# Two-layer hybrid decoder trunk on one core: gate-weight split inside the fixed first stage, a later gate chain, a value sum in SBUF, and convolutions without edge operations

## The chip, the cores and the metric

The kernel runs on one core of a Trainium2 chip. The metric is the device time of one execution in microseconds. Engines are named as in the profile: PE (TensorE matmul), PEld (its weight loads), DVE (VectorE), ACT (ScalarE), POOL (GpSimd), SP (SyncE, which issues most DMAs). L12 is line 12 of the kernel before the change.

## The reference, cut to what matters

Sequence 1024, model width 1024, two layers, all in float32. In each layer:

```python
shift, scale, gate = split(silu(c) @ w_ada + b_ada, 3)
h = rmsnorm(x, norm_g) * (1 + scale) + shift
mq, mk, mv, mo, mz, mi, mf, rq, rk, rv, rz = split_cols(h @ w_in)
qk = silu(causal_dwconv(concat(mq, mk), conv_w, conv_b))      # 4 taps along the sequence
y_m = sigmoid(mo) * layernorm(mlstm(qk, mv, mi + b_i, mf + b_f)) * silu(mz)   # 4 heads of 256
y_r = layernorm(retention(rotary(rq), rotary(rk), rv)) * silu(rz)             # 4 heads of 256
x = x + gate * (concat(y_m, y_r) @ w_out)
```

`mi` and `mf` are the input and forget gates: four columns each, 8 of the 9224 columns of `w_in`. A running maximum over the sequence of their cumulated logarithms scales the mLSTM heads. A final rmsnorm follows.

## The kernel before

**Precision.** Every float32 operand is split into a high part (a cast on ACT, `high` L399 or `split_to` L854) and a low part (a subtraction on POOL or DVE, `low` L404 or L855), and a product is three matmuls (`mm3`, L173 to L175).

**First stage.** The hidden rows `hT` are made tile by tile (8 tiles of 128 model columns, two halves of 512 tokens) and used at once by three blocks of 128 columns (`first`, L1473 to L1477). In layer 0 a script of short steps (L1481 to L1490) fixes the order of all engines: S, Q square sums of x; K scaling; T transposes; A one accumulation of the adaptive weights `w_ada` on DVE (L285, L287; A13 is group 1, row tile 3); P column sums; G gain and shift from them (L268 to L271); H the high part of a hidden tile (L1515, ACT), E its full value (L1521, ACT), U its low part (L1525, DVE); F and f the products with the high and the low part; W, w the split of weights. The loads of x, of the four groups of `w_ada` (L277) and of the three blocks stand on SP's queue in the order of use, and behind the last of them the gate weights (`gate_raw`, L476, tile `wgr`).

**Gates.** Behind the first stage `gate_units` (L480) makes the gate weights into a 36-column block: two zero fills (L485) and two high parts (L854) on ACT, two low parts (L855) on DVE, tiles cH and cL; then 48 matmuls. `gate_chain` (L495) turns the result into decays: some ACT functions, then 30 instructions of 4x512 on DVE (all of them, like the rotary tables', are shown as L140), eight transposes on PE (L554), and small work.

**Second stage, in slots.** The other columns go in pairs of blocks by Strassen's scheme with seven products, a11, S1, S2, a12, S4, S3, a22. `build_forms` (L612) makes the sums of hidden tiles that they need: U1 to U3 in four steps and, five ticks after the last of these, U4 in four more (L618 to L639, splits at L854 and L855). A pair of value heads (job v) has 14 slots, each product in two parts, in the order a12, a11, S2, S1, S3, a22, S4; a pair of z, query or key columns has 7 slots. The order of the jobs is the string `plan`. In a value pair (`vpair_product`, L769) the bank of a12 (pz, two of them) gets a11's product added (L803), and a store (L772) reads it from there: high part on ACT (L774), low part on DVE (L779), DMA. S1 takes the same two banks next. ACT copies of products (L754, L802, L808), sums and stores use twelve tiles named acc. Query and key pairs of the mLSTM heads go through `conv_chain` (L857): a scaled copy on ACT (L861), three multiply-adds on DVE (L867), for the second half of the tokens three more over the first 1 to 3 columns (L869) with the last three columns of the first half (`halo`, L863), then SiLU. Retention pairs are rotated (L940 to L942).

**What sets the order.** PE's order is the program's. On ACT, DVE, POOL and SP a planner lays each engine's order down when the program is built, by modelled times, and may take an instruction ahead of others that were written before it; it may also take one that was written behind the first stage into it. `late` pins an instruction behind what is written before it on its engine. Side work is written as generators that run in ticks, one tick per slot; `launch(gen, d)` starts one d ticks later and `yield n` puts it off by n. `gate_units` takes two ticks, the block behind it four, then slot 0 follows. The gate chain starts in the third tick and waits 7 ticks; its DVE work takes ten ticks, and its transposes come 13 ticks after the first of them. The attention of a head is launched 4 ticks after its keys, is one at a time, and lets the next one begin after 22 ticks (RELEASE, L964).

Of the kernel before, what the change touches and what calls it, by code (L numbers as in the profile page):

```python
# [19 lines left out]
P = 128  # L20
# [67 lines left out]
def tile_hybrid_trunk(ctx, tc, x, xt, c, positions, w_ada, b_ada, norm_g, w_in, w_blk, w_val, conv_w, conv_b,  # L88
# [16 lines left out]
    def nm(s):  # L105
        uid[0] += 1
        return f"{s}_{uid[0]}"
# [4 lines left out]
    def wt(tag, n, bufs, dt=F32):  # L112
        return wrk.tile([P, n], dt, tag=tag, bufs=bufs, name=nm(tag))

# [15 lines left out]
    def f(ap):  # L130
        return ap.bitcast(F32)

    def late(ins):
        tc.keep_in_program_order(ins)
        return ins
# [604 lines left out]

    def pair_product(F, done, loose=False):
        bank, keep = {}, {}

        def product(n, part, w):
            b, form = PRODUCT[n]
            new = b not in bank
            if new:
                bank[b] = ps_x() if b == "X" else ps_z()
            for k in range(4):
                mm3(bank[b], w[k], F[form][k], new and k == 0, k == 3, b != "Y")  # L750
            with tc.high_priority():
                if n in ("a11", "S1", "S2"):
                    keep[n] = wt("acc", 512, NACC)
                    A.copy(keep[n], bank[b])  # L754
                elif n == "a12":
                    c = keep["a11"] if loose else bank["Y"]
                    V.tensor_tensor(c, bank["Y"], keep["a11"], ALU.add)
                    done(0, 0, c)
                elif n == "S3":
                    V.tensor_tensor(keep["S1"], bank["X"], keep["S1"], ALU.add)  # L760
                    done(1, 1, keep["S1"])
                elif n == "S4":
                    V.tensor_tensor(keep["S2"], bank["Z"], keep["S2"], ALU.add)  # L763
                    done(0, 1, keep["S2"])
                else:
                    done(1, 0, bank["X"])
        return product

    def vpair_product(l, F, heads):  # L769
# [15 lines left out]
        def product(n, part, w):  # L785
# [13 lines left out]
            with tc.high_priority():  # L799
                if n == "a11":  # L800
                    c = wt("acc", 512, NACC)
                    A.copy(c, bank["X"])  # L802
                    V.tensor_tensor(bank["Y"], bank["Y"], c, ALU.add)  # L803
# [52 lines left out]

    def conv_chain(l, hg, which, m, half, pt, halo):  # L857
        cl = cols[l][0]
        ct = which * 8 + hg * 2 + m
        acc = wt("acc", 512, NACC)  # L860
        A.activation(acc, pt, AF.Identity, bias=cl[:, 8 + ct:9 + ct], scale=cl[:, 72 + ct:73 + ct])  # L861
        if half == 0:
            V.tensor_copy(halo, pt[:, HALF - 3:HALF])  # L863
        yield 1
        for d in range(1, 4):
            wcol = cl[:, 24 + 16 * (3 - d) + ct:25 + 16 * (3 - d) + ct]
            V.scalar_tensor_tensor(acc[:, d:], pt[:, 0:HALF - d], wcol, acc[:, d:], ALU.mult, ALU.add)  # L867
            if half:
                V.scalar_tensor_tensor(acc[:, 0:d], halo[:, 3 - d:3], wcol, acc[:, 0:d], ALU.mult, ALU.add)  # L869
        yield 1  # L870
# [46 lines left out]
    def conv_done(l, hg, which):  # L917
        halos = [wt("halo", 3, 4) for _ in range(2)]
        late = []

        def one(m, half, src, delay=0):
            launch(conv_chain(l, hg, which, m, half, src, halos[m]), delay)

        def done(m, half, src):
            if m and half:
                late.append(src)
                return
            one(m, half, src)
            if m:
                one(1, 1, late[0], 1)  # L930
        return done
# [425 lines left out]
    def norm_later(l, xn, sq, hT, half, keep, gaps):  # L1357
# [97 lines left out]
    for l in range(DEPTH):  # L1455
# [23 lines left out]
        if l == 0:  # L1479
# [10 lines left out]
            for step in script.split():  # L1490
# [59 lines left out]
            head_cols(0, hrows)  # L1550
            startup.__exit__(None, None, None)
        else:
            for half in range(2):
                for k in range(KT):
                    first(half, k)
                    tick()
                if half == 0:
                    drain()
        for half in range(2):
            z_evac(gp, 0)(half, pf[0][half])  # L1560
            o_evac(gp, 0, gdr[l][0])(half, pf[1][half])
            z_evac(gp, 1)(half, pf[2][half])
        if l == 0:
            for r in ring3:
                A.activation(r[:, :, HD:HD + 2], ident[:, 0:8].rearrange("p (a c) -> p a c", a=4), AF.Copy, scale=0.0)
                A.copy(r[:, 0:2, HD:HD + 1], rmask[:, 254:256].unsqueeze(2))
# [12 lines left out]
        plan = ("v45 v67 z4 q4 k4 z5 q5 k5 v01 q6 k6 q7 z6 k7 q0 a10 k0 v23 q1 k1 a11 q2 k2 q3 a20 k3 z7 a21 a30 a31",  # L1579
                "v45 q4 k4 z4 q5 k5 v67 q6 k6 z5 q7 k7 v01 q0 k0 z6 a10 q1 k1 v23 q2 k2 a11 q3 k3 a20 z7 a21 a30 a31")[l]  # L1580
        jobs = [(w[0], [int(d) for d in w[1:]]) for w in plan.split()]
# [17 lines left out]
        def job_product(what, arg):  # L1599
# [10 lines left out]
            if h > 3:  # L1610
                return pair_product(F, rot_done(l, h, which, *rot), True)
            return pair_product(F, conv_done(l, h, which))

# [86 lines left out]
```

## Time and profile before

| | |
|---|---|
| median of 3 runs | 2282.63 us (2281.71 to 2287.09) |
| the profiled execution | 2286.23 us |
| its span, first to last instruction | 2284.5 us |
| its granted PE clock, mean | 0.972 |
| busy: PE, DVE, ACT, POOL | 93%, 80%, 50%, 42% |
| DMA, mean | 196 GB/s |

The profile is one execution. Its waits name who ended an engine's idle time; a wait for several things is put down to the last. Rows of the timeline read: start and length in microseconds from the span's start, engine, line, operation, output<-inputs, shapes, count, and in brackets the idle time before it with who ended it. Rows by groups read: busy microseconds, mean nanoseconds of one, idle time before them.

### The profile page before, as it was taken

The page shows a single profiled execution, that of the slowest core. Times are in us where ns is not written, and L with a number is a line of the kernel's source. Part 1 is how long each engine was busy: PE and PEld are TensorE (multiplying, and loading weights), DVE is VectorE, ACT ScalarE, POOL GpSimd, SP SyncE. Part 2 cuts the span into 40 slices and gives each one's busy share as a digit, 9 for nine tenths or more (in the row PEclk, how much of TensorE's full clock was granted, in tenths as well). Part 3 has the DMA queues.
Part 4 walks back from the last instruction along what each step waited for, and adds up shares of the span by engine and source line. Part 5 has one row for each costly group of instructions (what it writes and reads, how often), then busy time and mean ns, then how long its engine had stood idle before and what let it go on. Part 6 is the DMA issues. An engine that isn't in the chain of part 4 may idle for free. (4 is left out here: it accounts for less than half of the span.)

```text
span 2284.5 us, 35248 instructions
## 1 busy us (share of the span) xinstructions
PE 2134.0 (93%) x11483; PEld 1840.7 (81%) x11483; DVE 1827.6 (80%) x3301; ACT 1150.6 (50%) x2157; POOL 957.2 (42%) x842
## 2 busy tenths in 40 slices
PE   5979899999999998999999799999999899899998
PEld 3778789878897877888787788988988888688887
DVE  5898888888979999893627989698697789977653
ACT  5634344444555656653456333544555555565442
POOL 0343244444354544514266434544635353442323
PEclk8999999999999999999999899999999999999999
DMA  8247678887686767686633676877867677576974
GB/s 261 66 116 217 192 233 228 237 240 190 180 244 166 191 183 188 194 268 212 215 126 79 201 197 194 245 193 204 245 159 207 183 205 196 155 205 198 261 256 118
DMA packets 452549, 448.32 MB, mean 196 GB/s; under 512 B 191218, under 2 KB 309754, under 8 KB 452364
## 3 DMA queue, kind: packets, MB, share of 16 engines
q1 hardware_dynamic: 432636, 410.14, 58.0%
q0 software_dynamic: 19584, 35.66, 10.4%
q8 instruction: 90, 1.47, 0.3%
q14 instruction: 95, 0.78, 0.1%
q10 hardware_dynamic: 144, 0.26, 0.0%
HBM read 322.69 MB, written 123.24 MB: 195 GB/s over the span
## 5 line engine op out<-in xcount | busy, mean ns | idle before, releaser
L399 ACT CAST wH<-R 128x512 fp32r<-128x512 f32 x616 | 378.2, 618 | 463.7 <-PE px L174 122.1
L404 POOL TENSOR_TENSOR R<-R,wH 128x512 fp32r<-128x512 f32 x276 | 395.9, 1441 | 508.1 <-ACT wH L399 344.2
L173 PE MATMUL px<-b,wH 128*128 128x512 f32 x912 | 365.1, 400 | 11.1 <-ACT acc L754 8.2
L174 PE MATMUL px<-b,wH 128*128 128x512 f32 x912 | 362.7, 398 | 0.0
L175 PE MATMUL px<-b,R 128*128 128x512 f32 x912 | 361.7, 397 | 0.0
L404 DVE TENSOR_TENSOR R<-R,wH 128x512 fp32r<-128x512 f32 x340 | 258.4, 764 | 112.3 <-ACT wH L399 107.5
L174 PE MATMUL pz<-b,wH 128*128 128x512 f32 x704 | 276.2, 392 | 5.1 <-DVE b L1251 5.1
L173 PE MATMUL pz<-b,wH 128*128 128x512 f32 x704 | 276.6, 393 | 1.9 <-DVE acc L763 1.8
L175 PE MATMUL pz<-b,R 128*128 128x512 f32 x704 | 275.3, 391 | 0.0
L173 PEld LDWEIGHTS px<-b,wH 128*128 128x128 f32 x912 | 176.0, 193 | 49.3 <-ACT acc L754 10.2
L175 PEld LDWEIGHTS px<-b,R 128*128 128x128 f32 x912 | 175.6, 193 | 38.4
L174 PEld LDWEIGHTS px<-b,wH 128*128 128x128 f32 x912 | 175.9, 193 | 34.1
L173 PE MATMUL px<-wH,b 128*128 128x256 f32 (+1 forms) x576 | 176.3, 306 | 18.3 <-DVE acc L867 6.3
L693 POOL DMA_DIRECT2D R<-in_w_blk_dram x104 | 92.4, 889 | 207.7 <-DMA R<-in_w_blk_dram 90.6
L174 PE MATMUL px<-R,b 128*128 128x256 f32 (+1 forms) x576 | 174.6, 303 | 4.2 <-DVE R L404 4.2
L175 PE MATMUL px<-wH,b 128*128 128x256 f32 (+1 forms) x576 | 174.2, 302 | 0.0
L174 PEld LDWEIGHTS pz<-b,wH 128*128 128x128 f32 x704 | 132.9, 189 | 31.4 <-DVE b L1251 6.4
L175 PEld LDWEIGHTS pz<-b,R 128*128 128x128 f32 x704 | 132.9, 189 | 28.4
L173 PEld LDWEIGHTS pz<-b,wH 128*128 128x128 f32 x704 | 132.9, 189 | 28.3 <-DVE acc L763 2.2
L173 PE MATMUL pz<-wH,b 128*128 128x256 f32 (+1 forms) x448 | 135.8, 303 | 17.3 <-DVE acc L779 16.0
L175 PE MATMUL pz<-wH,b 128*128 128x256 f32 (+1 forms) x448 | 135.2, 302 | 0.7 <-DVE b L1251 0.7
L174 PE MATMUL pz<-R,b 128*128 128x256 f32 (+1 forms) x448 | 135.1, 302 | 0.0
(359 smaller groups left out, 5346.7 us busy)
## 6 DMA issues: line engine op xcount, KB each, us to landing
R<-in_w_blk_dram SPq DMA_DIRECT2D x276, 256.0 KB
vdr<-acc SPq DMA_DIRECT2D x128, 256.0 KB
ring<-vdr SPq DMA_DIRECT2D x64, 512.0 KB
R<-in_w_out_dram SPq DMA_DIRECT2D x128, 256.0 KB
R<-in_w_blk_dram POOLq DMA_DIRECT2D x104, 256.0 KB, 4.5
R<-in_w_val_dram SPq DMA_DIRECT2D x80, 256.0 KB
gdr<-acc SPq DMA_DIRECT2D x64, 256.0 KB
acc<-in_w_ada_dram SPq DMA_DIRECT2D x64, 256.0 KB
```

The lines of the kernel that those rows point to most:

```text
L173: PE.matmul(o, lt[0], rt[0], start=start, stop=False, skip_group_check=more)
L174: PE.matmul(o, lt[0], rt[1], start=False, stop=False, skip_group_check=more)
L175: PE.matmul(o, lt[1], rt[0], start=False, stop=stop, skip_group_check=more)
L399: A.copy(h, r)
L404: eng.tensor_tensor(lo, r, f(h), ALU.subtract)
L693: G.dma_start(raw[n], src, accum_op=ALU.add)
```

## The change

1. The split of the gate weights becomes a function of its own, `gate_weights`. In layer 0 it is step X of the fixed first stage, between f04 and U05; in layer 1 it stands behind the first half's products, pinned, and its load ahead of them.
2. `gate_chain` waits 12 ticks instead of 7, and layer 1's plan has z4 ahead of q4 and k4.
3. In a value pair the sum of a12 and a11 is written to the acc tile of a11's copy instead of the bank, and the store reads it there.
4. The kept tiles of a pair have three more columns in front; the halo is copied there, so that the convolution's three multiply-adds run over the second half in one piece and L869 goes. All acc tiles are 516 columns instead of 512.
5. Small: the fills of the value ring's last columns are pinned behind the first stage, the products of `norm_later` are pinned in the first half, and `late` does nothing inside the fixed first stage.

```diff
     def wt(tag, n, bufs, dt=F32):
-        return wrk.tile([P, n], dt, tag=tag, bufs=bufs, name=nm(tag))
+        t = wrk.tile([P, 516 if tag == "acc" else n], dt, tag=tag, bufs=bufs, name=nm(tag))
+        return t[:, 0:n] if tag == "acc" else t
...
-    def gate_units(gr, hT, pgs):
+    def gate_weights(gr):
         wg = (wt("cH", 516, 1, F32R)[:, 0:KT * 36], wt("cL", 516, 1, F32R)[:, 0:KT * 36])
...
         for w in w3:
-            A.activation(w[:, :, 4:32], ones.unsqueeze(1).to_broadcast([P, KT, 28]), AF.Copy, scale=0.0)
+            late(A.activation(w[:, :, 4:32], ones.unsqueeze(1).to_broadcast([P, KT, 28]), AF.Copy, scale=0.0))
         for a, b in ((0, 4), (32, 0)):
-            split_to((w3[0][:, :, a:a + 4], w3[1][:, :, a:a + 4]), gr3[:, :, b:b + 4], V)
+            late(A.copy(w3[0][:, :, a:a + 4], gr3[:, :, b:b + 4]))
+            late(V.tensor_tensor(w3[1][:, :, a:a + 4], gr3[:, :, b:b + 4], f(w3[0][:, :, a:a + 4]), ALU.subtract))
+        return wg
+
+    def gate_units(wg, hT, pgs):
...
-        yield 7
+        yield 12
...
+        def halo(n, pt):
+            if conv:
+                V.tensor_copy(full[n][:, 0:3], pt[:, HALF - 3:HALF])
...
                 if n in ("a11", "S1", "S2"):
-                    keep[n] = wt("acc", 512, NACC)
+                    full[n] = wt("acc", 515, NACC)
+                    keep[n] = full[n][:, 3:515]
...
-                    V.tensor_tensor(bank["Y"], bank["Y"], c, ALU.add)
-                    launch(store(part, 0, 0, bank["Y"]))
-                    del bank["Y"]
+                    V.tensor_tensor(c, bank["Y"], c, ALU.add)
+                    launch(store(part, 0, 0, c))
...
-    def conv_chain(l, hg, which, m, half, pt, halo):
+    def conv_chain(l, hg, which, m, half, pt):
...
-        if half == 0:
-            V.tensor_copy(halo, pt[:, HALF - 3:HALF])
...
-            V.scalar_tensor_tensor(acc[:, d:], pt[:, 0:HALF - d], wcol, acc[:, d:], ALU.mult, ALU.add)
-            if half:
-                V.scalar_tensor_tensor(acc[:, 0:d], halo[:, 3 - d:3], wcol, acc[:, 0:d], ALU.mult, ALU.add)
+            e = 0 if half else d
+            V.scalar_tensor_tensor(acc[:, e:], pt[:, o + e - d:o + HALF - d], wcol, acc[:, e:], ALU.mult, ALU.add)
...
-            V.tensor_tensor(xn[k], xn[k], R, ALU.mult)
+            (V if half else Later()).tensor_tensor(xn[k], xn[k], R, ALU.mult)
...
-                      "H14 f04 U05 E14 ...
+                      "H14 f04 X U05 E14 ...
...
+                elif what == "X":
+                    wg = gate_weights(vgr)
...
+            gr = gate_raw(l)
             for half in range(2):
                 for k in range(KT):
                     first(half, k)
                     tick()
                 if half == 0:
                     drain()
+                    wg = gate_weights(gr)
...
-        run_units(gate_units(gate_raw(l) if l else vgr, hT, pgs))
+        run_units(gate_units(wg, hT, pgs))
...
-                "v45 q4 k4 z4 q5 ...
+                "v45 z4 q4 k4 q5 ...
```

More of the change, by code (lines that the diff above doesn't have):

```diff
@@ L739, in vpair_forms, with pair_product @@
         return add
-    def pair_product(F, done, loose=False):
-        bank, keep = {}, {}
+    def pair_product(F, done, loose=False, conv=False):
+        bank, keep, full = {}, {}, {}
+        def halo(n, pt):
+            if conv:
+                V.tensor_copy(full[n][:, 0:3], pt[:, HALF - 3:HALF])
         def product(n, part, w):
@@ L757, in product @@
                     V.tensor_tensor(c, bank["Y"], keep["a11"], ALU.add)
+                    halo("S2", c)
                     done(0, 0, c)
@@ L760, in product @@
                     V.tensor_tensor(keep["S1"], bank["X"], keep["S1"], ALU.add)
-                    done(1, 1, keep["S1"])
+                    done(1, 1, full["S1"] if conv else keep["S1"])
                 elif n == "S4":
                     V.tensor_tensor(keep["S2"], bank["Z"], keep["S2"], ALU.add)
-                    done(0, 1, keep["S2"])
+                    done(0, 1, full["S2"] if conv else keep["S2"])
                 else:
+                    halo("S1", bank["X"])
                     done(1, 0, bank["X"])
@@ L860, in conv_chain @@
         acc = wt("acc", 512, NACC)
[L861 to L863 removed]
+        o = 3 * half
+        A.activation(acc, pt[:, o:o + HALF], AF.Identity, bias=cl[:, 8 + ct:9 + ct], scale=cl[:, 72 + ct:73 + ct])
         yield 1
@@ L917, in conv_done @@
     def conv_done(l, hg, which):
-        halos = [wt("halo", 3, 4) for _ in range(2)]
-        late = []
+        late_one = []
         def one(m, half, src, delay=0):
-            launch(conv_chain(l, hg, which, m, half, src, halos[m]), delay)
+            launch(conv_chain(l, hg, which, m, half, src), delay)
         def done(m, half, src):
             if m and half:
-                late.append(src)
+                late_one.append(src)
                 return
@@ L929, in done @@
             if m:
-                one(1, 1, late[0], 1)
+                one(1, 1, late_one[0], 1)
         return done
```

14 lines of the change are left out of this document (9 added, 5 removed), and 2 rows, old and new, of the table script.

## The prediction

> **What bounds the kernel now.** The first view is the page's first part, busy time by engine.
>
> ```profile
> PE 2134.0 (93%) x11483; PEld 1840.7 (81%) x11483; DVE 1827.6 (80%) x3301; ACT 1150.6 (50%) x2157; POOL 957.2 (42%) x842
> ```
>
> PE is busy for 93% of the span of 2284.5 us, so about 150 us of it are idle. The work of PE itself isn't touched by the change; only its idle time can go. So the second view is the list of waits of PE (what waited, for whom, us in total, times, longest).
>
> ```profile
> PE pz L173 <- DVE acc L779: 16.0, 3, 7.6
> PE pa L175 <- DVE b L909: 15.3, 7, 5.3
> PE pz L1473 <- ACT b L1515: 12.9, 1, 12.9
> ...
> PE px L173 <- ACT acc L754: 8.2, 3, 5.2
> ...
> PE px L173 <- DVE acc L867: 7.8, 4, 5.5
> ...
> PE px L173 <- DVE acc L810: 4.8, 2, 4.6
> PE pa L554 <- DVE cL L140: 4.0, 1, 4.0
> ```
>
> One wait of 12.9 us is a single event. The third view, the timeline of ACT, DVE and PE about it (start, length, what; in brackets the idle time before it), tells whose it is.
>
> ```profile
> 28.34 3.17 ACT L371 ACTIVATE b<-b,rs 128x512 f32<-128x512 f32 x5 [0.54 <-POOL rs L1354]
> 45.40 0.34 ACT L854 CAST cH<-wgr 128x32 fp32r<-128x32 f32 x2 [13.89 <-DMA wgr<-in_w_in_dram]
> 45.65 0.77 ACT L1515 ACTIVATE b<-pa,gsh 128x512 fp32r<-128x512 f32 x1
> ```
>
> ```profile
> 33.56 0.48 DVE L285 TENSOR_SCALAR b<-b,cact 128x512 f32<-128x512 f32 x1 [1.48 <-DMA b<-in_w_ada_dram]
> 45.65 0.31 DVE L855 TENSOR_TENSOR cL<-wgr,cH 128x32 fp32r<-128x32 f32 x2 [11.61 <-ACT cH L854]
> ...
> 47.12 0.69 DVE L1525 TENSOR_TENSOR b<-acc,b 128x512 fp32r<-128x512 f32 x1 [0.49 <-ACT acc L1521]
> ...
> 53.73 0.48 DVE L285 TENSOR_SCALAR b<-b,cact 128x512 f32<-128x512 f32 x1
> ```
>
> ```profile
> 33.17 0.40 PE L1477 MATMUL pa<-b,q 128*128 128x512 f32 x1
> 46.47 0.80 PE L1473 MATMUL pz<-b,wH 128*128 128x512 f32 x1 [12.90 <-ACT b L1515]
> ...
> 52.56 0.48 PE L1473 MATMUL pz<-b,wH 128*128 128x512 f32 x1
> ```
>
> ACT stood still from 31.51 to 45.40 with the cast of the gate weights at its head, an instruction that nothing in the first stage needs, because their load `wgr` had not landed. Behind it in ACT's queue stood the casts of the hidden rows for PE (L1515), and DVE stood behind the matching subtraction. That is a stall by order, not by work.
>
> The fourth view is a table by stage (length; busy time of PE, PEld, DVE, ACT and POOL; granted clock; DMA).
>
> ```profile
> 52.60:83.40 30.80, 30.80 (x154) 25.73 (x155) 24.22 (x43) 22.35 (x35) 4.87 (x4) 1.00 0.31 77
> 46.40:51.40 5.00, 4.93 (x15) 3.96 (x15) 2.92 (x5) 4.19 (x8) 0.00 (x0) 0.50 0.50 117
> 139.50:144.80 5.30, 5.25 (x26) 5.28 (x27) 5.24 (x10) 1.24 (x2) 1.61 (x2) 0.54 0.61 173
> 1267.10:1274.80 7.70, 7.65 (x50) 7.68 (x51) 7.70 (x8) 1.83 (x3) 4.82 (x4) 0.76 0.80 208
> 1285.00:1293.80 8.80, 8.75 (x50) 8.78 (x51) 8.69 (x15) 2.42 (x5) 0.88 (x1) 0.65 0.83 235
> 1307.60:1312.20 4.60, 4.59 (x14) 3.60 (x15) 4.52 (x9) 0.77 (x2) 0.16 (x1) 0.63 0.82 207
> 83.50:245.40 161.90, 136.19 (x888) 120.69 (x886) 149.34 (x269) 69.97 (x118) 65.15 (x47) 0.94 0.53 144
> 1218.50:1400.00 181.50, 163.12 (x851) 138.39 (x850) 170.34 (x225) 79.35 (x137) 88.46 (x60) 0.93 0.58 166
> ```
>
> From 52.6 to 83.4, the rest of the first stage, PE is never idle. After it, up to 245.4, DVE is busy for 149.3 of 161.9 us, more than PE's 136.2; from the same place of layer 1 on (1218.5 to 1400) it has DVE at 170.3 of 181.5, PE at 163.1. So the second stage of either layer is bound by DVE's queue, and whatever the change moves there can win no more than DVE's idle time. The short windows show a second price of a gap: after each long wait the granted clock is at 0.50 to 0.76 for some microseconds.
>
> **The change part by part.**
>
> **Gate weights (step X, gate_weights).** The two casts and two subtractions now stand in the fixed order behind f04, so ACT goes from L371 at 31.51 straight to L1515. I work out when PE would be where it was at 52.56. DVE, free at 34.04, needs an accumulation, the low part L1525 and a second accumulation, some 0.7 us each (L1525 0.69; the accumulation between 45.96 and 47.12 - 0.49 took 0.67): 36.1. PE, out of work at 33.57, has thirteen instructions until then (at 30.80/154 = 0.20 us in the mean of 52.6 to 83.4, some 2.6 us) and then the eight column sums of the accumulation, which start at 36.2 and take about 1 us; so it stands there at 37.1, a gain of 15.4. What is late next? The loads that follow.
>
> ```profile
> 27.82 11.60 SPq L277 DMA_DIRECT2D b<-in_w_ada_dram  x16
> 39.80 0.37 SPq L476 DMA_DIRECT2D wgr<-in_w_in_dram  x1
> ```
>
> The 16 tiles of groups 2 and 3 are issued from 27.82 at a pitch of 0.73 us. The first was what DVE waited for until 33.56, and wgr (issued 39.80) landed at 45.40: some 5.7 us each from issue to use. The first tile of group 3, the ninth, is issued at 33.6 and lands near 39.3; DVE used it at 53.73 and would now want it at 38.3. That costs 1 us; later tiles are needed later than they land. X itself comes at some 54 us, behind the landing of wgr at 45.4, and adds no wait for it; on DVE U05 queues behind X's subtraction, which waits for ACT's casts, and I count 0.4 us. **Term: -14** (bounds -11.6, DVE's own idle time, to -15.4). The zero fills and ring fills of ACT, which stood in its idle start, cost under 2 us of an engine with 8 us free in 52.6 to 83.4: nothing. In layer 1 the same four casts stand behind the first half's products; the high rows of the second half queue behind them on ACT for about 1.2 us; PE needs these rows one after the other, so I count nothing, at worst 1.2.
>
> **First value sum in SBUF, and gate chain behind the forms.** The two act at one place, the value pair v45 of each layer.
>
> ```profile
> 120.67 0.69 DVE L803 TENSOR_TENSOR pz<-pz,acc 128x512 f32<-128x512 f32 x1
> 124.66 0.69 DVE L803 TENSOR_TENSOR pz<-pz,acc 128x512 f32<-128x512 f32 x1
> 128.04 0.68 DVE L779 TENSOR_TENSOR acc<-pz,acc 128x512 fp32r<-128x512 f32 x1
> 132.03 0.67 DVE L140 SCALAR_TENSOR_TENSOR q<-q,dm 4x512 f32<-4x512 f32 x1
> 138.74 0.67 DVE L779 TENSOR_TENSOR acc<-pz,acc 128x512 fp32r<-128x512 f32 x1
> 175.25 1.65 DVE L140 TENSOR_TENSOR cL<-cf,zt 4x512 f32<-4x512 f32 x1
> ```
>
> ```profile
> PE pz L173 <- DVE acc L779: 10.2, 2, 7.6
> ```
>
> S1 takes the two pz banks of a12. Before, a bank comes free at L779 (128.72 and 139.41); after, at the end of L803 (121.36 and 125.35), earlier than S1 wants it. Of the 16.0 us for L779, 10.2 fall between 83.5 and 245.4, in layer 0 (the last row), and 5.8 in layer 1. With the slow clock behind the second (46% of 5.3 = 2.4) the gross in layer 0 is 12.6. The gate chain's 30 DVE instructions (the first at 132.03, the last at 175.25) move from slots 3 to 12 to slots 8 to 17, and its transposes (L554) from behind slot 16 to behind slot 21: so the second form sums (U4) and S3's sum (L810) no longer queue behind it. But its work isn't less. The ceiling is DVE's idle time up to the rotary products, 161.9 - 149.3 = 12.6.
>
> ```profile
> L140 DVE CAST acc<-acc 128x256 fp32r<-128x256 f32 x4 | 2.2, 557 | 8.3 <-DMA rdr<-acc 8.3
> ```
>
> 8.3 us of that idle time are waits of the rotary tables for their own stores; the later gate chain fills those. **Term, layer 0: -8** (0 to -12.6). Layer 1: gross 5.8 + 4.6 (L810, ahead of 1285) + at most 8.2 - 5.2 = 3.0 (L754, ahead of 1307), and by the clock 24% of 7.7, 35% of 8.8 and 37% of 4.6 = 6.6, in all 20.0; the ceiling from 1218.5 to 1400 is 181.5 - 170.3 = 11.2. Putting z4 ahead of q4 and k4 hands the chain a stretch with less DVE work (no rotary products, no key transposes). Head 4's attention starts 7 slots later, at slot 39; it holds the next one off for 22 slots, to 61, where k5 has been waiting since 53, and the queue has caught up by head 0 (127 against 130). **Term: -6** (0 to -11.2).
>
> L779 now reads two SBUF tiles in 16 more cases (two value parts of eight pairs), a form that takes 679 ns in the second row below; L618, also with two, takes 1095 in the mean. So 0 to 16 x 0.42 = 6.7 us of DVE; I take 0, the row of the same line.
>
> ```profile
> L618 DVE TENSOR_TENSOR acc<-b,b 128x512 f32<-128x512 f32 x40 | 41.9, 1095 | 0.0
> ...
> L779 DVE TENSOR_TENSOR acc<-acc,acc 128x512 fp32r<-128x512 f32 x16 | 10.8, 679 | 0.0
> ```
>
> The Trainium skill, SBUF — State Buffer, section Who interferes with whom, speaks against this edit: it says that a DVE instruction with two SBUF inputs contends with a GpSimd instruction that reads SBUF, and one with a single SBUF input doesn't. L618 fits it (1095 ns, beside POOL's splits), L779 with two inputs (679 ns) doesn't show it. With every one of the 16 held up like L618, an estimate by that page, the sum below would be 26 instead of 33.
>
> **Convolutions.** The 96 edge instructions of L869 go.
>
> ```profile
> L869 DVE SCALAR_TENSOR_TENSOR acc<-halo,cols,acc 128x1 f32<-128x1 f32 (+2 forms) x96 | 37.2, 388 | 0.0
> ```
>
> That is 37.2 us of DVE, over two stretches in which PE waits for DVE now and then (L867 7.8, L909 15.3). The halo copies stay, 32 as before, at another place; full-width L867 gains at most 3 columns of 512. DVE is not the bound there, so only a part comes through: a quarter of those 23.1 us is 5.8. **Term: -5** (0 to -12). The kept tiles start 12 bytes in; L867 writes at such offsets already (acc[:, d:]), so I count nothing. norm_later's pinned products keep an order that they have.
>
> **Sum:** 14 + 8 + 6 + 5 = 33. The profiled run took 2286.23 us (span 2284.5), so 2253.2 on its own time; it stands 3.6 above the median of 2282.63, which makes **2250**.
>
> **The rivals.** *DVE takes it back* (2268): the stages that follow the first are DVE's, the moved work returns as waits at L554 and at the rotary tables, and a sum held in SBUF needs one of twelve acc tiles for longer. For it: DVE's 170.3 of 181.5 us. Then only the 14 us of the first stage stay: 2282.6 - 14 = 2268.6, between 2260 and 2275. *DVE's idle time fills whole* (2233): 14 + 12.6 + 11.2 + 12 = 49.8, between 2226 and 2242; against it, its idle waits are partly DMA. *The acc tile* (slower): the sum's tile is held from L803 to L779, 7 and 14 us in v45. Such a tile is late already:
>
> ```profile
> 244.78 0.59 ACT L754 COPY acc<-px 128x512 f32<-128x512 f32 x1 [3.56 <-DMA rdr<-acc]
> ```
>
> ACT's copy waits there until a store lets go of an acc tile, and PE behind it for 5.2 us, the longest of its waits for L754. If each of four of the eight value pairs costs 5.2 + 2.4 (clock), 30.4, and the terms of 8 and 6 don't come, 2282.6 - 19 + 30.4 = 2294; it ends slower once four pairs lose over 4.8 us each. Against it: the sum's tile was taken before too, only for a shorter time. *The change doesn't do what it says* (2271): the order is a plan, and another early cast takes the place of the gate weights at ACT's head, such as that of the next block's weights, whose issue followed at 47.09 and which by the same 5.7 us would land near 52.8; ACT would wait 7.3 us longer than now: 2282.6 + 7.3 - 19.
>
> **How the numbers follow.** Forecast 2250, own range 2242 to 2260: 0.52. DVE takes it back: 0.20. Idle time fills whole: 0.13. The acc tile: 0.07. Not what it says: 0.04. No change: 0.04. The range, 2236 to 2273, holds the forecast, most of the second, the fifth and near half of the third, 8 in 10. About 0.3% (6.8 us) is what a measurement of this kernel can tell from no change; faster than that are the forecast and the second, third and fifth case, 0.89; within it 0.04; slower 0.07.
>
> **What would show it.** The cast of cH from wgr at about 53 us without a wait, PE's 12.9 us wait gone, the first stage's end at 69 to 70 instead of 83.5 (if not, the first term is wrong); no wait of pz for L779, and instead L803 writing acc; if the second term fails, waits of L554 of over 8 us, or ACT copies waiting for acc. Layer 1's products of 1260 to 1300 without its gaps; no L869, and DVE's busy time some 37 us less. The forecast is wrong if ACT is held in the first stage by something else, or if the wins up to 245 come back as waits by 400.

## The result, and the profile after

| | before | after |
|---|---|---|
| median of 9 runs each | 2281.71 us | 2269.46 us |
| ratio, with its 95% interval | | 0.9944, 0.9928 to 0.9959 |
| the profiled execution | 2286.23 us | 2268.18 us |
| its span, granted PE clock | 2284.5 us, 0.972 | 2266.5 us, 0.979 |

The change makes the kernel 12 us (0.56%) faster. The forecast was 33 us on the profiled execution, 32 on the medians: the direction held, the time lies in the range (2236 to 2273), but most of the gain isn't there, and the time is that of the rival *DVE takes it back* (2268). The experiments show that it got there in another way than that rival says.

The first view of the profile after is the page's first part, busy time by engine.

```profile
PE 2151.5 (95%) x11483; PEld 1832.0 (81%) x11483; DVE 1817.5 (80%) x3205; ACT 1159.4 (51%) x2163; POOL 964.3 (43%) x842
```

PE's idle time went from 2284.5 - 2134.0 = 150.5 us to 2266.5 - 2151.5 = 115.0: that is 35.5 less, what the forecast asked for. But with the same 11,483 matmuls, PE is busy for 17.5 us more. This is the line to stop at: half of what the waits gave is eaten by the matmuls. And DVE is busy for 10.1 us less, where 37.2 us of edge instructions had gone. That figure is to be read with care: with no change of its work at all (before_pad256 below, 1833.1 for 1827.6) DVE's busy time moves by 5.5 us.

The second view is the list of PE's waits (us in total, times, longest).

```profile
PE px L177 <- DVE acc L824: 12.3, 2, 7.4
PE pa L1114 <- POOL sL L1071: 10.2, 6, 3.5
PE px L177 <- ACT acc L817: 9.3, 5, 3.0
PE px L1547 <- DMA b<-in_w_ada_dram: 8.3, 1, 8.3
PE pa L562 <- DVE cL L144: 7.4, 2, 4.4
PE px L177 <- ACT acc L767: 7.4, 4, 5.4
...
PE pa L177 <- ACT n L1144: 4.6, 1, 4.6
PE px L177 <- DVE acc L881: 4.1, 1, 4.1
...
PE pa L179 <- DVE b L921: 3.6, 4, 1.6
```

The wait for the gate weights (12.9) is gone, the waits of pz for L779 (16.0) are gone, those for the convolutions' multiply-adds (L867) and for the low part of the attention's keys (L909) fell from 7.8 and 15.3 to 4.1 and 3.6 (L881, L921). New or longer are S3's value sum (L824, 4.8 before as L810), a low part on POOL in the attention (L1071, 5.7 before as L1060), ACT's copies in the value pairs (L817, 5.6 before as L802), the gate chain's transposes (L562, 4.0 before as L554), and one for n (L1144).

The third view is the timeline at the place of the first term.

```profile
33.16 0.78 ACT L1526 ACTIVATE b<-pa,gsh 128x512 fp32r<-128x512 f32 x1 [0.57 <-PE pa L382]
...
55.49 0.33 ACT L491 CAST cH<-wgr 128x32 fp32r<-128x32 f32 x2
```

```profile
71.76 0.39 PE L1488 MATMUL pa<-b,q 128*128 128x512 f32 x1
```

ACT goes on with the hidden rows at 33.16 and comes to the gate weights at 55.49 without a wait. The last matmul of the first stage (the third row) started at 83.24 before and starts at 71.76: 11.5 us earlier.

### The profile page after: what moved, and what is told of

Its sections match the earlier page's. It is cut to its first block, busy times and chain, and to the rows that moved or that the text cites. A ratio compares the mean times of both kernels' runs of the same rounds, so it can differ in the third digit from the quotient of the medians.

```text
span 2266.5 us, 35156 instructions
## 1 busy us (share of the span) xinstructions
PE 2151.5 (95%) x11483; PEld 1832.0 (81%) x11483; DVE 1817.5 (80%) x3205; ACT 1159.4 (51%) x2163; POOL 964.3 (43%) x842
## 4 chain that ended last, share of the span: by engine, by line
PE 57%; DVE 22%; DMA 10%; issue 5%; POOL 2%; ACT 2%; SPq 1%; DVEq 0%; POOLq 0%; ACTq 0%
PE px L177 8%; PE px L178 8%; PE px L179 8%; PE pz L179 6%; PE pz L178 6%; PE pz L177 6%; PE pa L177 4%; PE pa L179 4%; PE pa L178 4%; DVE acc L881 3%; DVE R L408 2%; PE pa L1123 2%; DVE acc L626 2%; DMA acc<-kfr 1%; PE pa L1032 1%
## 5 line engine op out<-in xcount | busy, mean ns | idle before, releaser
L177 PE MATMUL px<-b,wH 128*128 128x512 f32 x912 | 364.8, 400 | 8.2 <-ACT acc L767 7.4
L178 PE MATMUL pz<-b,wH 128*128 128x512 f32 x704 | 280.2, 398 | 1.3 <-DVE b L1262 1.3
L179 PE MATMUL pz<-b,R 128*128 128x512 f32 x704 | 281.0, 399 | 0.0
L177 PE MATMUL pz<-b,wH 128*128 128x512 f32 x704 | 279.8, 397 | 0.2 <-ACT acc L767 0.2
L177 PEld LDWEIGHTS px<-b,wH 128*128 128x128 f32 x912 | 174.6, 191 | 48.1 <-ACT acc L767 8.9
L177 PE MATMUL px<-wH,b 128*128 128x256 f32 (+1 forms) x576 | 177.7, 309 | 27.4 <-DVE acc L824 12.3
L177 PEld LDWEIGHTS pz<-b,wH 128*128 128x128 f32 x704 | 133.8, 190 | 29.4 <-ACT acc L767 0.6
L177 PEld LDWEIGHTS px<-wH,b 128*128 128x128 f32 x576 | 115.5, 201 | 32.2 <-ACT acc L817 10.4
L177 PE MATMUL pz<-wH,b 128*128 128x256 f32 (+1 forms) x448 | 134.0, 299 | 0.0
```

What stands on the lines that cost most here:

```text
L177: PE.matmul(o, lt[0], rt[0], start=start, stop=False, skip_group_check=more)
L178: PE.matmul(o, lt[0], rt[1], start=False, stop=False, skip_group_check=more)
L179: PE.matmul(o, lt[1], rt[0], start=False, stop=stop, skip_group_check=more)
```

## The experiments

All ratios are against the kernel before, run on the same chip in the same rounds, with a 95% interval. Lines (L177) are those of the kernel that a row is from, so one line of the program has several numbers.

**One part at a time on the kernel before.** The diffs are those of the change, one part each: step X with the pinned order; the convolutions with the wider tiles; the value sum with `yield 12`; the order of the second layer.

**x_only.** Expected:

> The kernel before with the gate weights' split alone (step X behind f04, in layer 1 behind the first half's products, the pinned order of the ring fills and of the first half's xn x R). Theory A (the first stage's gain is real, what the second stages' edits free is taken back by DVE): PE's wait of 12.9 us at 52.6 gone, layer 0's first stage 11 to 13 us shorter, the whole -11 to -14, so nearly all of the 12 measured for the full change. Theory B (all parts but one are worth what was forecast, one is a loss): -14 as well, but then the other single parts must show theirs. Theory C (a gain in an early stage is partly given back in any later stage, whatever the part): only -4 to -8 at the end although the first stage ends 11 to 13 us earlier.

Measured: 2265.72, ratio 0.9919 (0.9894 to 0.9943), 18 us faster. One part brings at least what the whole change brings (0.9944; the intervals overlap), and more than the 11 to 14 of the theories.

**conv_only.** Expected:

> The kernel before with the convolutions without edge operations alone (acc tiles 516 wide, halo copied ahead of the kept sum). DVE's busy time falls by up to 37 us. Theory A: PE waits for little of it, -1 to -4. Theory B with this part as forecast: -5 to -8; theory B with this part as the loss (the sum tiles' halo copy is one more DVE step ahead of the first chain and the wider tiles change the plan): +3 to +8.

Measured: 2278.05, ratio 0.9982 (0.9965 to 1.0), 4 us, with an interval that reaches to no change. DVE's busy time is 1796.2, 31 less than before.

**vy_only.** Expected:

> The kernel before with the first value sum in SBUF and the gate chain's later slot (yield 12 for 7) alone. Theory A: PE's waits for L779 go in both layers, and new waits for S3's sum, the gate chain's transposes and ACT's copies take most of it: 0 to -4. Theory B with this part as forecast: -10 to -14; as the loss: +3 or more.

Measured: 2286.47, ratio 1.0019 (1.0005 to 1.0034), 4 us slower. In its trace the 800th matmul of PE starts 8.0 us earlier than before (183.1 to 175.1), the size of the prediction's term. But only part of that is won. Two rows of PE show what stands there now.

```profile
145.18 0.58 PE L173 MATMUL px<-wH,b 128*128 128x256 f32 x1 [6.69 <-DVE acc L809]
...
191.21 1.12 PE L554 MATMUL pa<-ident,cL 128*128 128x128 f32 x4 [4.40 <-DVE cL L140]
```

The two waits for L779 (10.2) have gone, and one of 6.69 for S3's sum (L809 here) has come: at the 700th matmul 3.8 us are won. The other 4 are the wait for the gate chain's transposes, which before lay ahead of the 800th matmul (3.99 at 177) and now lies behind it. How much is left later is best read against the trace of before_pad256, which is the kernel before with an unused tile and as fast (below); the profiled execution of the kernel before itself fell 5.0 us behind that one by the 5000th matmul, without any difference in work. Against it vy_only is 7.4 us ahead at the 800th matmul, 0.9 at the 1200th (about 260 us) and 0.1 at the 5000th. In the second layer 6.3 come by the 6400th and are gone by the 6800th, within 100 us.

**plan_only.** Expected:

> The kernel before with the second layer's order alone (z4 ahead of q4 and k4, v67 behind k5). Theory A: -2 to +2. Theory B with this part as the loss: +4 to +10, with a slower stretch between 1400 and 1800 as in the full change (PE's 361.6 busy us there became 372.3, at a granted clock of 0.98 for 1.00).

Measured: 2297.81, ratio 1.0055 (1.0033 to 1.0076), 13 us slower. The rows show where; the first is PE's, the others are ACT's just before it.

```profile
1570.95 0.58 PE L173 MATMUL pa<-ring,b 128*128 128x256 f32 x1 [6.09 <-ACT n L1133]
```

```profile
1570.00 0.62 ACT L854 CAST kc<-acc 128x512 fp32r<-128x512 f32 x1 [7.87 <-DMA acc<-kfr]
1570.53 0.64 ACT L1133 COPY n<-pa 128x256 f32<-128x256 f32 x2
```

A cast of the attention's keys stands at the head of ACT's queue with its load not landed, and n, for which PE waits, stands behind it: the same stall by order as the gate weights' in the first stage. A second loss follows at 1668, 4.20 us for the low part of keys on DVE (L909). The kernel before has no wait of PE of over 0.9 us in this stretch (1426 to 1733). The change has the first of the two as well (its 4.6 us for L1144). So the second layer's order is a loss, as theory B allowed for one part; but the value sum is one too, and the four singles add up to 18.5 + 4.1 - 4.3 - 12.6 = 5.7 us faster, less than the whole change. Neither theory had that.

**The parts together.** Each kernel is the change less what is named.

**x_conv, without the value sum, the later gate chain and the new order.** Expected:

> The changed kernel without the value sum in SBUF, without the later gate chain and with the old order of the second layer: the gate weights' split and the convolutions without edge operations alone. The single parts measured against the kernel before: -17 (2265.72 for 2282.84), -4.8 (2278.05), the value sum with the gate chain +3.6 (2286.47), the second layer's order +15 (2297.81). Theory A2 (the parts add up, and two of the four are losses): 2282.8 - 17 - 5 = 2261, so about 8 us faster than the full change's 2269.5. Rival (the parts only work together, since the full change took 12 off where the sum of the four singles is -3): 2266 to 2270, no better than the gate weights alone.

Measured: 2253.65, ratio 0.9872 (0.9854 to 0.9891), faster than the 2261 of theory A2.

**x_conv_v, the same with the value sum.** Expected:

> Gate weights, convolutions and the value sum in SBUF, with the gate chain at its old slot and the old order of the second layer. Against x_conv it shows the value sum alone. Theory A2: the waits for L779 (8 us by the profile in layer 0, as many in layer 1) go and come back as waits for the gate chain that stands ahead of S3's sum: -3 to +2 against x_conv. Rival (what gives the gain back is the gate chain's new slot): -8 to -14 against x_conv.

Measured: 2258.36, ratio 0.9898 (0.988 to 0.9917): 5 us above x_conv by the medians, where theory A2 had at most 2 and the rival a gain.

**no_plan, the change with the old order.** Expected:

> The changed kernel with the second layer's old order (q4 k4 ahead of z4). Theory A2: the order costs 10 to 15 here as alone: 2255 to 2262. Rival (the order is a loss only beside the old value sum, whose wait it moves, and is neutral in the full change): 2268 to 2272.

Measured: 2267.24, ratio 0.9924 (0.9904 to 0.9945), between the two expectations.

**no_vy, the change with the sum in PSUM and `yield 7`.** Expected:

> The changed kernel with the first value sum back in PSUM and the gate chain back at yield 7 (old slot). Theory A2: 2 to 5 faster than the full change, 2264 to 2268. Rival (the new order needs the freed banks): slower than the full change, 2272 to 2282.

Measured: 2262.62, ratio 0.9923 (0.9902 to 0.9943), a little faster than theory A2's 2264.

So x_conv, half of the change, is 16 us faster than the whole (0.9872 for 0.9944, intervals apart). The single steps from it to the change (0.9872, 0.9898, 0.9924, 0.9944) are 4.6 to 5.9 us each, of which each alone is about as large as its interval; together they aren't in doubt. no_vy shows that the order costs about as much beside the old value sum (0.9923 for 0.9872) as the value sum with the later gate chain costs beside the old order (0.9924 for 0.9872). If the two added in full, the change would stand at 0.9975; that it stands at 0.9944 is a difference of the size of the intervals.

What the value sum does is seen at one place, in PE's timeline of x_conv and of x_conv_v.

```profile
117.23 0.55 PE L177 MATMUL pz<-wH,b 128*128 128x256 f32 x1 [2.64 <-DVE acc L794]
127.90 0.55 PE L177 MATMUL pz<-wH,b 128*128 128x256 f32 x1 [6.19 <-DVE acc L794]
```

```profile
137.83 0.58 PE L177 MATMUL px<-wH,b 128*128 128x256 f32 x1 [10.68 <-DVE acc L824]
```

Two waits of 8.8 us are gone, and one of 10.7 stands ten microseconds on. The view by windows says why: first the same place in the kernel before (from PE's 400th matmul on), then in x_conv and x_conv_v.

```profile
111.40:150.00 38.60, 26.20 (x194) 25.36 (x193) 38.30 (x48) 14.46 (x27) 23.61 (x15) 0.87 0.36 106
```

```profile
100.00:140.00 40.00, 29.21 (x203) 28.32 (x202) 39.19 (x50) 15.45 (x28) 23.38 (x15) 0.83 0.39 125
```

```profile
100.00:139.00 39.00, 26.13 (x206) 25.16 (x205) 38.69 (x47) 15.30 (x28) 23.37 (x15) 0.88 0.37 110
```

The fourth column is DVE: 38.30 of 38.60 us, 39.19 of 40.00, 38.69 of 39.00. DVE has no free time there in any of them, so a wait that goes returns at the next instruction in its queue.

The later gate chain meets the same queue further on. no_plan is x_conv_v with `yield 12`, and the place is where PE first waits for ACT's copy L767; the first row is PE's, the second ACT's.

```profile
231.18 0.79 PE L177 MATMUL px<-b,wH 128*128 128x512 f32 x1 [7.07 <-ACT acc L767]
```

```profile
230.54 0.58 ACT L767 COPY acc<-px 128x512 f32<-128x512 f32 x1 [4.92 <-DVE acc L307]
```

ACT's copy waits for DVE's L307 (a step of the second layer's adaptive weights) to be done with an acc tile, and in DVE's queue the rotary tables' instructions and the gate chain's last steps stand ahead of it. The wait of PE is 7.07 us in no_plan and 5.40 in the change, and 1.0 to 2.0 in x_conv, x_conv_v and no_vy, which have the old slot. no_plan is 8.0 us ahead of x_conv_v at PE's 800th matmul and 2.3 behind at the 1200th.

**Where PE's busy time comes from.** In the traces, a product's matmuls of 512 columns start 226 to 227 ns apart in every kernel without the convolutions' edit and 232 to 235 ns in every kernel with it, from the first product to the last, also where no convolution is near. What the edit changes for all of them is an address: twelve acc tiles of 516 columns for 512 (which take 2080 bytes each for 2048) push wH, the tile that holds the high part of PE's weights, up by 384 bytes, with all that lies behind it. R (their low part) and b (the hidden rows) lie ahead of acc and stay, so of what these matmuls read only wH moves. The test needs no other edit:

```
+    gap = []
     def wt(tag, n, bufs, dt=F32):
+        if tag == "wH" and not gap:
+            gap.append(wrk.tile([P, 96], F32, tag="gap", bufs=1, name="gap"))
```

**before_pad384.** Expected:

> The kernel before, the same instructions in the same order, with an unused tile of 384 bytes a partition allocated ahead of wH: wH then lies where the wider acc tiles of the change put it (byte 193472 of a partition for 193088), everything ahead of it stays. In the traces every kernel without the convolutions' edit starts a 512-wide pair product's matmuls 226 to 227 ns apart, every kernel with it 232, 232 and 235 ns. Theory S (the wider acc tiles shift wH, the matmuls' weights, to an address at which matmuls are slower): 232 to 235 ns here too, and with some 5,000 such matmuls 6 to 8 ns each about 25 to 33 us of PE time more; at the end, where part of that falls into waits, +12 to +30 (2295 to 2312). Theory T (the slower matmuls come from acc itself, its odd addresses or the copies into it): 227 ns and no change, 2278 to 2287.

Measured: 2291.65, ratio 1.0042 (1.0024 to 1.0059), 9.6 us slower, with 232, 233 and 235 ns between the matmuls of a product. The steps are those of theory S; the time is less than the 12 to 30 that it had for the end.

**x_conv_pad512, x_conv with 32 columns in place of the 96.** Expected:

> x_conv (gate weights and convolutions, 2253.65) with an unused tile of 128 bytes ahead of wH, which moves wH by 512 bytes in all against the kernel before in place of 384 (byte 193600), with acc as wide and as odd as in the change. Theory S, if the address counts within 512 bytes or less: matmuls back at 227 ns and the time 12 to 30 lower, 2224 to 2242. Theory T: 232 to 235 ns and 2251 to 2256.

Measured: 2247.27, ratio 0.9846 (0.9821 to 0.9871); 227 ns. It is short of the 12 us that theory S had at least.

**after_pad512.** Expected:

> The whole change with the same 128 bytes ahead of wH. Theory S: 227 ns and 2240 to 2258, which is where the prediction put the change (2250). Theory T: as the change, 2264 to 2275.

Measured: 2257.6, ratio 0.9898 (0.9873 to 0.9923), for the change's 0.9944: 10.5 us back; 227 ns.

**before_pad256, with 64 columns.** Expected:

> The kernel before with 256 bytes ahead of wH (byte 193344). It tells apart two forms of theory S. If what counts is wH's place within 256 bytes (64 as before; 192 in the change): 227 ns, 2278 to 2287. If it is the place within 512 bytes or more (64 before, 320 here, 448 in the change): slower matmuls, +5 to +30. Theory T: 227 ns and no change.

Measured: 2283.44, ratio 1.0003 (0.9987 to 1.0019); 227 ns.

**before_pad64B, with 16 columns.** Expected:

> The kernel before with an unused tile of 64 bytes ahead of wH (byte 193152; its place within 256 bytes is 128, for 64 with the fast and 192 with the slow address). If only wH's place within 128 bytes against the other operands', or any other place than theirs, costs: 232 to 235 ns and +5 to +15. If the slow case is half of 256 bytes alone: 227 ns and no change.

Measured: 2295.35, ratio 1.0062 (1.004 to 1.0084); 233 to 234 ns. Theory T has fallen, theory S holds: wH at 64 past a multiple of 256 bytes, where R and b lie too, costs nothing, at 128 and at 192 it costs 5 to 8 ns a matmul. In the timeline of PE this is seen only over a dozen rows; first the change, then the change with 128 bytes more.

```profile
218.74 0.40 PE L179 MATMUL px<-b,R 128*128 128x512 f32 x1
...
221.54 0.40 PE L179 MATMUL pz<-b,R 128*128 128x512 f32 x1
```

```profile
218.18 0.39 PE L183 MATMUL px<-b,R 128*128 128x512 f32 x1
...
220.90 0.39 PE L183 MATMUL pz<-b,R 128*128 128x512 f32 x1
```

From the first row to the second are twelve steps, with no wait: 2.80 us or 233 ns each, and 2.72 us or 227 ns. The trace has 3 x 1744 such matmuls; 232, 233 and 235 ns for 227 are 6.3 in the mean, or some 33 us. Not all of it reaches the end. The page's first parts, of before_pad384 and of after_pad512:

```profile
PE 2154.4 (94%) x11483; PEld 1834.9 (80%) x11483; DVE 1825.1 (80%) x3301; ACT 1151.6 (50%) x2157; POOL 948.9 (41%) x842
```

```profile
PE 2122.8 (94%) x11483; PEld 1830.7 (81%) x11483; DVE 1825.7 (81%) x3205; ACT 1157.2 (51%) x2163; POOL 971.9 (43%) x842
```

PE's busy time in before_pad384 is 20.4 us above that of the kernel before (2134.0). Its span is 2290.0 us, so PE is idle for 135.6, for 150.5 before: 15 us come out of waits, as would be if the other engines catch up with a slower PE. Its clock is granted at 0.976 for 0.972, 0.4% of the span or 9 us, which would be about the rest of the 33; that is arithmetic, not an experiment.

**conv_pad512.** Expected:

> The convolutions' edit alone (conv_only, 2278.05 for 2282.84), with 128 bytes ahead of wH, so that its matmuls run at 227 ns again. From before_pad384, where the slow address alone cost 9.7, and conv_only's -4.8: -10 to -20, 2262 to 2272. If the convolutions' edit has little worth of its own: 2275 to 2282.

Measured: 2263.68, ratio 0.992 (0.9892 to 0.9948): 18 us, for the 4 of conv_only, so wH's place costs 14 here. In its list of waits these are left, for 7.8 (L867) and 15.3 (L909) before:

```profile
PE px L178 <- DVE acc L879: 4.3, 2, 4.0
PE pa L180 <- DVE b L919: 4.3, 4, 1.5
```

The profiled execution is the fastest of this kernel's six (2253.27), but the two waits are as short in x_conv_pad512 (4.0 and 4.2) and in the change (4.1 and 3.6).

**Does free time on DVE let the value sum's gain through?** Two kernels with x_conv and the 128 bytes cut the gate chain's DVE instructions to 64 of 512 columns; most gates are left out, and the exponentials of the chain have a scale of 0.

```
-            V.tensor_tensor_scan(bq[0:4], on4[0:4], lfq[0:4], prev.get("bq", 0.0), ALU.mult, ALU.add)
+            V.tensor_tensor_scan(bq[0:4, W], on4[0:4, W], lfq[0:4, W], prev.get("bq", 0.0), ALU.mult, ALU.add)
```

**light.** Expected:

> x_conv with wH moved back to a fast address (x_conv_pad512, 2247.27), and with the gate chain's DVE instructions cut from 512 columns to 64 (the gates of most positions are left out, so the output is not the reference's; the exponentials have a scale of 0). It takes some 20 us of DVE work out of the second stage of either layer. It is the base for light_v; by itself, if DVE bounds these stages, 2225 to 2242; if not, 2245 to 2250.

Measured: 2227.35, ratio 0.9766 (0.974 to 0.9792). DVE's busy time falls by 36.6 us (1816.3 to 1779.7) and the time by 18 (0.9766 for 0.9846): these stages are DVE's.

**light_v.** Expected:

> light with the first value sum in SBUF. Beside the full gate chain the same edit cost 4.7 (2258.36 for 2253.65): PE's waits of 2.64 and 6.19 us for L794 went and one of 10.68 for L824 (S3's sum) came right behind. Theory D (DVE has no free time there, so a wait that goes returns at the next instruction in its queue): with free time the sum's gain stays, -4 to -12 against light. Rival E (the sum's own costs, the acc tile held longer and the DVE form with two SBUF inputs, eat the gain): 0 to +6 against light.

Measured: 2232.79, ratio 0.9795 (0.9769 to 0.9821): no gain, and by the medians 5 us slower, as rival E has it (0 to +6). As theory D put it, it has failed. The traces of light and of light_v show that the test missed its place:

```profile
125.44 0.55 PE L181 MATMUL pz<-wH,b 128*128 128x256 f32 x1 [4.60 <-DVE acc L800]
```

```profile
135.46 0.58 PE L181 MATMUL px<-wH,b 128*128 128x256 f32 x1 [8.19 <-DVE acc L830]
```

```profile
100.20:136.70 36.50, 26.52 (x203) 26.12 (x202) 36.12 (x58) 14.99 (x28) 23.82 (x15) 0.89 0.41 124
```

Up to 136.7 DVE is busy for 36.12 of 36.50 us in light_v even so: the forms' sums and the weights' low parts fill it, and the lighter chain frees DVE only behind. So the wait went to S3 again (7.3 us in all for L800 in light, 8.2 for L830 in light_v). Rival E has a row of its own, in the groups of the change (busy us, mean ns):

```profile
L794 DVE TENSOR_TENSOR acc<-acc,acc 128x512 fp32r<-128x512 f32 x32 | 28.6, 903 | 1.9 <-DMA kdr<-acc 1.6 <-DVE acc L894 0.3
```

Before, the same 32 instructions took 10.8 + 10.8 = 21.6 us, 16 of them with an input in PSUM. The timelines of DVE and of POOL show one of them:

```profile
116.60 1.77 DVE L794 TENSOR_TENSOR acc<-acc,acc 128x512 fp32r<-128x512 f32 x1
```

```profile
116.08 3.44 POOL L408 TENSOR_TENSOR R<-R,wH 128x512 fp32r<-128x512 f32 x2
```

Of the 32, 24 take 0.65 to 0.69 us and eight take 0.89 to 1.81; each of the eight lies beside a subtraction of POOL with two inputs in SBUF. It isn't always DVE that waits: six of the 24 lie beside one for practically their whole time, and there POOL's takes 1.82 to 4.19 us, where 1.30 is the median for 512 columns. (L618's 1095 ns in the prediction are the mean of two such groups as well, 0.67 to 0.70 us and 1.15 to 1.78.) This is the rule of the Trainium skill that the prediction weighed (SBUF — State Buffer, Who interferes with whom) and then priced at nothing: the estimate by it was 6.7 us of DVE, the row says 7.0. The price depends on what POOL does at the time: in x_conv_v the same line takes 25.8 us for 22.5 in x_conv, so 3.3.

**What the gate weights are worth where.** Both leave the second layer's split behind the forms.

**x_first, pinned there (`wg = gate_weights(gate_raw(l))` ahead of gate_units).** Expected:

> The kernel before with the gate weights' split in the first layer's fixed stage alone; the second layer's split stays where it was, and the ring fills and xn x R keep their old freedom. If the first stage's 12 us are what it brings: -11 to -14 (2268 to 2271), and the other 4 to 6 of x_only's 17 come from the second layer's part and the pinned order (in x_only's trace a wait of 3.5 us for L1258 near 1100 us and one of 3.3 for R near 1393 are gone). If what follows the first stage moves by itself with the shift: -16 to -19.

Measured: 2273.83, ratio 0.9966 (0.995 to 0.9982). That is 8 us, short of the 11 to 14 expected. It is no clean test: the pinned split makes two waits of its own.

```profile
1208.65 0.42 PE L176 MATMUL pa<-b,cH 128*36 128x512 f32 x1 [3.02 <-ACT cH L490]
1211.60 0.64 PE L178 MATMUL pa<-b,cL 128*36 128x512 f32 x1 [2.30 <-DVE cL L491]
```

**x_first2, not pinned.** Expected:

> The kernel before with the gate weights' split in the first layer's fixed stage, and the second layer exactly as before, not pinned. x_first's trace is 12 to 13 us ahead up to 1138 us, then loses 8 to its own waits for the split. If that loss is x_first's own: -12 to -14 here (2267 to 2270). If the first stage's gain is partly taken back in any case: -6 to -10.

Measured: 2269.08, ratio 0.995 (0.9933 to 0.9967), 11 us by the ratio and 12.4 by the medians. That is the first stage's share. The other 7 of x_only's 18.5 would be the second layer's split and the pinned order; the intervals of the two overlap by a hair (0.9933 and 0.9943), so it is likely rather than shown.

## Why the prediction was right and wrong

In the order in which the parts can be added, by the ratios: gate weights -18.5 (0.9919), the convolutions with wH at its old place -16.6 (0.9846), wH's place +5.9 (0.9872), the value sum +5.9 (0.9898), the gate chain's slot +5.9 (0.9924), the second layer's order +4.6 (0.9944). The forecast had -14, -5, 0, and -14 for the last three. Each of the last four steps is about as large as its interval, and they depend on the order: in the whole change wH's place costs 10.5.

- **Gate weights, -14: right, and short.** The mechanism held at every row that the prediction named: no wait at the cast, 11.5 us at the end of the first stage (just below the bounds of 11.6 to 15.4; 69 to 70 was forecast, 72 came). So the first stage gave less than forecast, and that the whole part gave more is not by the mechanism named: what was counted at nothing, layer 1's split and the pinned order, may bring another 7.
- **Value sum and gate chain, -8, and layer 1, -6: wrong sign; the step that failed is the ceiling.** "The ceiling is DVE's idle time up to the rotary products, 161.9 - 149.3 = 12.6" is an average over 162 us. The free time lies behind; from 111 to 150 us, where v45 stands, DVE was busy for 38.30 of 38.60. With the value sum alone, 8.8 us of waits become one of 10.7 (x_conv_v). With the later gate chain 8 us come by 175 us, and by about 260 us they are gone: half were the transposes' wait, put off, and where the convolutions' edit is in, ACT's copy L767 waits longer by 3 to 6 us. On top of it comes the price of the form with two SBUF inputs, 3.3 to 7.0 us of DVE, taken at 0 because the 16 such instructions of the same line took 679 ns: 14 of those lie beside no subtraction of POOL for more than a tenth of their time, and beside the other two (at 219 and 406 us) it was POOL's that took longer, 2.38 and 1.76 us. The rival *DVE takes it back* had this part right.
- **The second layer's order, a share of the -6: wrong sign.** The step that failed is "the queue has caught up by head 0", by which the attention's later start was to cost nothing. In the new order a load's cast stands ahead of n in ACT's queue, and PE loses 6.1 us at 1571, and 4.2 for DVE at 1668. That head 4's later start is what puts it there is likely, but wasn't tried by itself.
- **Convolutions, -5: right sign, size a third.** The term took a quarter of PE's 23.1 us of waits for L867 and L909, because DVE is not the bound there. 14.5 of the 23.1 went (8.6 left in conv_pad512). The waits here didn't shrink in proportion to how full DVE is: with 37 us less work in the queue ahead of them, most of them went. What makes up the few us between 14.5 and the 16.6 to 18 of the time isn't shown.
- **The wider tiles, 0: the step that nobody would look for.** "The kept tiles start 12 bytes in ... so I count nothing" thought of the tiles themselves. Their width moved another tile, and that cost 5.9 to 14 us of the end and some 33 us of PE's steps.

The forecast missed since two terms were too small, two had the wrong sign, and one was not on the list; that the time is the rival's 2268 is a sum of errors. Of the rival, the moved work that returns is shown; that "only the 14 us of the first stage stay" is not: the convolutions' 17 came too and were eaten by the losses. A loss by the longer hold of the sum's acc tile, as in the rival *The acc tile*, isn't shown: the copy L767 that waits for such a tile waits for DVE's queue, and among the kernels with the convolutions' edit it waits long only with the later gate chain. What stays open is how the value sum's loss divides between the moved wait and the DVE form with two inputs: light and light_v don't tell them apart.

x_conv_pad512 is faster than both kernels: 2247.27, ratio 0.9846 (0.9821 to 0.9871), 35 us below the kernel before and, by the ratios, 22 below the change. It is the gate weights, the convolutions and 128 unused bytes.

## What to carry to other kernels

Ask for the free time of the bounding engine at the place where the wait stands, not over the stage: a wait that goes at a full queue comes back at the next instruction of that queue. Undo a change of several parts one by one; half of this one is better than the whole. When PE's busy time moves and the number of its matmuls doesn't, look at the step from start to start of a dozen of them, and at what a new tile size does to the addresses of the tiles behind it.

## What the runs showed of the hardware

- The place of the weights' tile within 256 bytes sets the step of 512-column fp32r matmuls: 227 ns with wH at 64 (as R and b), 232 to 235 at 128 and 192. Moves of 256 and 512 bytes change nothing. Matmuls of 256 columns show no such step (117 to 121 ns in every kernel). Whether what counts is the place itself or its distance from the moving operand's place wasn't tried.
- A matmul that is 3% slower costs far less than its sum: some 33 us of PE's steps became 10 at the end (before_pad384; 6 to 14 in the other three pairs), with 15 us less idle time and a granted clock of 0.976 for 0.972.
- Where a DVE instruction with two inputs in SBUF meets such a subtraction of POOL, one of the two takes longer: DVE's up to 1.81 us for 0.68, or POOL's up to 4.19 for 1.30.
